# A gated encoder block on one core: root formula, order of the first tiles' products and sharing of the first weights' casts changed

## The chip, the cores and the metric

The kernel runs on one core of a Trainium2 chip. Its engines are named as the profile names them: PE (matrix products, with PEld loading their stationary operand), DVE (vector), ACT (scalar and activations), POOL (GpSimd) and SP (which only issues transfers). The metric is the device time of one execution in microseconds (us). Before the change three runs took 900.99, 902.10 and 902.17 us; their median is 902.1 us.

## The reference

One layer with 1024 tokens and 1024 features: a norm, one wide projection, a window attention branch, a spatial gating branch, two gates, an output projection and a last norm.

```python
def rmsnorm(x, g):
    y = xf * lax.rsqrt(jnp.mean(xf * xf, axis=-1, keepdims=True) + EPS)
    return (y * g.astype(jnp.float32)).astype(x.dtype)

h = rmsnorm(x, norm_g[l])
proj = h @ w_in[l]
q, k, v, za, u, vs, zs, gm = jnp.split(proj, IN_SPLITS, axis=-1)
...
a = (a * jax.nn.silu(za)) @ w_att_out[l]
sgo = chunked_spatial_gating(gelu(u), gelu(vs), sg_w[l], sg_b[l], sg_ln_g[l], sg_ln_b[l])
sgo = (sgo * jax.nn.silu(zs)) @ w_sg_out[l]
ga, gs = jnp.split(jax.nn.sigmoid(gm + b_merge[l]), N_BRANCHES, axis=-1)
x = x + (ga * a + gs * sgo) @ w_o[l]
...
return rmsnorm(x, final_g)
```

## The kernel before

**Products.** Every fp32 factor is split in two parts: a high part (an fp32r copy, made by a cast) and a low part (the source minus the high part, made by a subtraction). A product is then three PE products: high by high, high by low and low by high. On top of that, matrices are cut in 2x2 blocks and multiplied with seven block products in place of eight. That needs sums of weight blocks (`s1` to `s4`) and sums of token blocks (`b11`, `b21`, `t1` and so on).

**The head.** The first stage computes the block `vs` of the projection, with tokens on the partitions. There are eight tiles of 128 tokens. Tiles 0 to 3 go through `first_tile`, tiles 4 to 7 through `second_tile`. For each tile:

- `load_x` brings the tile by a transfer on SP's queue. Tiles 0, 1, 2, 5, 6 and 7 share three buffers `wr`, tiles 3 and 4 lie in `T_t1l`; a later tile's load waits until an earlier tile has left its buffer.
- `scale_of` sums the squares on ACT and calls `rstd_of`, which makes the reciprocal root: a scaled mean on DVE, a root on ACT, a reciprocal and then one step of refinement on DVE.
- `turned_half` scales one half of the tile on DVE (`scalings`) and turns it with four PE transposes into a bank `ps_sc`.
- `form_of` casts the bank into the high part on ACT (`casts`) and subtracts the low part on DVE (`lows`).
- `first_product` issues 24 products of 128x512: twelve of `b11` with the weight block `a11` (bank `ps_mm` or `ps_tp`) and twelve of `b21` with `a12` (bank `ps_o`). Then ACT copies the second bank.

**The first weights.** `a11` and `a12` come in two chunks each (c = 0 to 3), each of two halves of 512 columns. `split_vs` makes their high and low parts. Before the change ACT casts both halves of chunk 0 and all of chunk 3, and POOL casts chunks 1 and 2; DVE subtracts, but for one half of chunk 0, which POOL subtracts.

**The sums of weights.** The blocks `s1`, `s2` and `s4` are made by transfers that add to their destination (`add_on`), issued by POOL: first on `T_t4h`, which becomes `s1`, in two chunks, then on `T_t3h` (`s2`) and `T_t3l` (`s4`), each from the one before. `split_behind` casts and subtracts `s1` into `T_t2h` and `T_t2l`, one cast for each chunk of 1024 columns.

**Order.** A scheduler puts the instructions of each engine into one sequence, which the engine then follows strictly. `after(second, first)` adds an edge that the scheduler must keep; it makes no wait of its own when both stand on one engine. `behind` and `paced` make a real wait. `keep_busy(n)` issues n products on constant data ahead of the first transposes.

**The end.** The last stage multiplies by `w_o`, adds the residual and applies the last norm with `rstd_of`. Its last root uses the option `times_minus_2`, which leaves out one step and takes a gain that was scaled by -0.5 (`g_last`).

Of the kernel before, what the change touches and what calls it, by code (L numbers as in the profile page):

```python
# [24 lines left out]
F32 = mybir.dt.float32  # L25
# [27 lines left out]
def hybrid_tile(  # L53
# [51 lines left out]
    eps_sb = const.tile([P, 1], F32, name="eps_sb")  # L105
    nc.gpsimd.memset(eps_sb[:], EPS)
    zeros = [nc.gpsimd.memset(g_both[:, at : at + 2, :].bitcast(F32), 0.0) for at in (0, 2)]
# [25 lines left out]

    def rstd_of(ss, scale, base=EPS, n=1, times_minus_2=False):

        ve = mtile([P, n], F32, f"st{n}", 16 if n == 1 else 5)
        of_mean.append(nc.vector.tensor_scalar(ve[:], ss, scale, base, op0=ALU.mult, op1=ALU.add))
        rt = mtile([P, n], F32, f"st{n}", 16 if n == 1 else 5)
        of_root.append(nc.scalar.activation(rt[:], ss, AF.Sqrt, bias=eps_sb[:] if base is EPS else base, scale=scale))
        r0 = mtile([P, n], F32, f"st{n}", 16 if n == 1 else 5)  # L140
        nc.vector.reciprocal(r0[:], rt[:])
        e = mtile([P, n], F32, f"st{n}", 16 if n == 1 else 5)
        if n == 1:
            nc.vector.scalar_tensor_tensor(e[:], ve[:], r0[:], r0[:], op0=ALU.mult, op1=ALU.mult)
            if times_minus_2:
                nc.vector.scalar_tensor_tensor(e[:], e[:], 3.0, r0[:], op0=ALU.subtract, op1=ALU.mult)
                return e
        else:
            nc.vector.tensor_mul(e[:], ve[:], r0[:])
            nc.vector.tensor_mul(e[:], e[:], r0[:])  # L150
        nc.vector.tensor_scalar(e[:], e[:], -0.5, 1.5, op0=ALU.mult, op1=ALU.add)
        nc.vector.tensor_mul(e[:], e[:], r0[:])
        return e
# [418 lines left out]
    for n in range(2):  # L572
        for half in range(2):
            spread(n, half)
    keep_busy(9)

# [57 lines left out]
    def form_of(name, t, src, minus=False):  # L634
# [6 lines left out]
        else:  # L641
            casts.append(nc.scalar.copy(hi, src))
            lows.append(nc.vector.tensor_sub(lo, src, hi.bitcast(F32)))

    def split_behind(hi, lo, src):
        after(nc.scalar.copy(hi, src), casts[-1])
        after(nc.vector.tensor_sub(lo, src, hi.bitcast(F32)), lows[-1])

# [67 lines left out]
    def split_vs(c):  # L716
        name = "a11" if c < 2 else "a12"
        raw = two_k(raws[name], c % 2)
        if c < 3:
            hi, lo = pair_of_w()  # L720
        else:
            hi, lo = (mtile([P, D], F32R, "s", 2) for _ in range(2))
        if c in (1, 2):

            for k in range(2):
                nc.gpsimd.tensor_copy(hi[:, half_of(k)], raw[:, k, :])
            first_lows.append(nc.vector.tensor_sub(lo[:], flat(raw), hi[:].bitcast(F32)))  # L727
        elif c:
            first_lows.append(split(hi[:], lo[:], flat(raw)))
        else:  # L730

            for k in range(2):
                ks = half_of(k)
                after(nc.scalar.copy(hi[:, ks], raw[:, k, :]), of_root[0])
                first_lows.append(
                    (nc.gpsimd if k else nc.vector).tensor_tensor(
                        lo[:, ks], raw[:, k, :], hi[:, ks].bitcast(F32), op=ALU.subtract
                    )
                )
        keep_w(name, c % 2, hi, lo)  # L740

    def vs_product(acc, name, t, weight, fresh, last=True, cs=(0, 1), terms=(0, 1, 2)):
        bh, bl = hb[name]
        for c in cs:
            for n in terms:
                for k in (2 * c, 2 * c + 1):
                    wh, wl = vs_w[weight, k]
                    lt = (bh, bh, bl)[n][:, k, tokens(t)]
                    rt = (wh, wl, wh)[n]
                    mm = nc.tensor.matmul(  # L750
                        acc[:],
                        lt,
                        rt,
                        start=fresh and k == 0 and n == 0,
                        stop=k == 3 and n == terms[-1],
                        skip_group_check=True,
                    )
        return mm

    accs = {}  # L760
    t5s = {}

    def first_product(t):
        accs[t] = bank("mm" if t < 2 else "tp")
        m2 = bank("o")
        if t:
            vs_product(accs[t], "b11", t, "a11", True)
            vs_product(m2, "b21", t, "a12", True)
        else:
            vs_product(accs[t], "b11", t, "a11", True, cs=(0,))  # L770
            vs_product(accs[t], "b11", t, "a11", False, cs=(1,), terms=(0, 2, 1))
            vs_product(m2, "b21", t, "a12", True, terms=(0, 2, 1))
        nc.scalar.copy(x_place(0, 0, t), m2[:])

# [3 lines left out]
    def by_s1(t):  # L778
        t5s[t] = bank("o" if t < 2 else "sc")
        mm = vs_product(t5s[t], "t1", t, "s1", True)  # L780
        nc.scalar.mul(x_place(1, 1, t), t5s[t][:], -1.0)
        return mm
# [4 lines left out]
    def keep_t5(t):  # L787
        nc.scalar.copy(x_place(0, 1, t), t5s[t][:])

# [5 lines left out]
    x_in[1] = load_x(1)  # L795
    first_lows = []
# [23 lines left out]
    for c in (2, 3):  # L820
        split_vs(c)
        after(first_lows[c + 1], lows[1])
    after(hi_of[0], casts[1])
    for move in unsplit:
        after(move(), hi_of[0])
    for c in range(2):
# [25 lines left out]
    mm = by_s1(0)  # L852
    load_part("s3", "t4h", 1, 0, mm)
    a22 = [raw_tile(), mtile([P, D], F32, "s", 2)]
# [19 lines left out]
    after(second_tile(6), move)  # L874
    mm = by_s1(1)
    after(second_tile(7), move)
# [19 lines left out]
    split_w("s2", 1)  # L896
    for t in range(4):
        keep_t5(t)

# [981 lines left out]
    g_both = bq()  # L1881
    g_out, g_last = g_both[:, 0:2, :], g_both[:, 2:4, :]
    nc.sync.dma_start(g_out.rearrange("p h n -> p (h n)"), final_g.partition_broadcast(P))
# [7 lines left out]
    for p in range(4):  # L1891
# [10 lines left out]
        def add_and_square(i, half, src, sign):  # L1902
            z = xr[:, 2 * i + half, :]
            pace[0] = (nc.vector.tensor_sub if sign < 0 else nc.vector.tensor_add)(z, z, src)
            ss = mtile([P, 1], F32, "st1", 16)
            nc.scalar.activation(bank("tp")[:], z, AF.Square, accum_out=ss[:])
            if p == 3 and i == half:
                scaled[i, half] = mtile([P, HALF], F32, gtag(), 1, pool)
                gain = (g_last if i else g_out)[:, half, :]
                nc.gpsimd.tensor_tensor(scaled[i, half][:], z, gain, op=ALU.mult)  # L1910
            if i in sq:
                sq[i] = rstd_of(ss[:], 1.0 / D, sq[i][:])
            else:
                nc.vector.tensor_scalar(ss[:], ss[:], 1.0 / D, EPS, op0=ALU.mult, op1=ALU.add)
                sq[i] = ss

        def scale_and_store(i, p=p, t=t, xr=xr, sq=sq, scaled=scaled):
            r = sq[i]
            row = slice((t + i) * P, (t + i + 1) * P)
            for e in range(2):  # L1920
                z = xr[:, 2 * i + e, :]
                if (i, e) in scaled:
# [5 lines left out]
                    continue  # L1928
                gain = (g_last if p == 3 and i else g_out)[:, e, :]
                by_gain = nc.vector.scalar_tensor_tensor(z, z, r[:], gain, op0=ALU.mult, op1=ALU.mult)  # L1930
# [8 lines left out]
        product(acc, ready[n, 3], ob["t2"], False)  # L1939
        copied = nc.scalar.copy(x12[:], acc)  # L1940
        if p == 2:
            after(nc.scalar.mul(g_last, g_out, -0.5), copied)
        if p:
# [44 lines left out]
        for e in range(2):  # L1988
# [7 lines left out]
            if e == 0:  # L1996
                base = mtile([P, 1], F32, "st1", 16)
                nc.vector.scalar_tensor_tensor(base[:], ss[:], 1.0 / D, sq[1][:], op0=ALU.mult, op1=ALU.add)
            else:
                sq[1] = rstd_of(ss[:], 1.0 / D, base[:], times_minus_2=True)  # L2000
        scale_and_store(0)
# [84 lines left out]
```

## Time and profile before

| what | value |
|---|---|
| median of three runs | 902.1 us (900.99 to 902.17) |
| the profiled execution: its time, its span | 900.83 us, 899.0 us |
| around the span (the difference) | 1.8 us |
| busy: PE, PEld, DVE, ACT, POOL | 890.0, 745.2, 683.5, 529.5, 153.6 us |
| granted PE clock, mean | 0.998 |
| from the start to the first transpose's load | 8.13 us |
| first product of tile 0, first product of tile 1 | 9.63 us, 17.26 us |
| last product's end to the end of the span | 892.48 to 899.0 us |

How to read it: the page gives for each engine the time in which it was busy. The timeline gives start, length, engine, line, operation and shape of each group of instructions, and in square brackets how long the engine had been idle and what released it. The chain of waits is followed back from the last instruction. Products on PE overlap, so that one lasts longer (some 0.39 us) than the distance between two of them.

### The profile page before, as it was taken

The page shows a single profiled execution, that of the slowest core. Times are in us where ns is not written, and L with a number is a line of the kernel's source. Part 1 is how long each engine was busy: PE and PEld are TensorE (multiplying, and loading weights), DVE is VectorE, ACT ScalarE, POOL GpSimd, SP SyncE. Part 2 cuts the span into 40 slices and gives each one's busy share as a digit, 9 for nine tenths or more (in the row PEclk, how much of TensorE's full clock was granted, in tenths as well). Part 3 has the DMA queues.
Part 4 walks back from the last instruction along what each step waited for, and adds up shares of the span by engine and source line. Part 5 has one row for each costly group of instructions (what it writes and reads, how often), then busy time and mean ns, then how long its engine had stood idle before and what let it go on. Part 6 is the DMA issues. An engine that isn't in the chain of part 4 may idle for free.

```text
span 899.0 us, 13239 instructions
## 1 busy us (share of the span) xinstructions
PE 890.0 (99%) x4306; PEld 745.2 (83%) x4306; DVE 683.5 (76%) x1248; ACT 529.5 (59%) x1062; POOL 153.6 (17%) x218
## 2 busy tenths in 40 slices
PE   9999999999999999999999999999999999999997
PEld 6888888888888888888888888888888888888885
DVE  7859966666687788888878888647797488479986
ACT  7866533334445567677777776755585376467453
POOL 4322222203030001111210111101121121110012
PEclk9999999999999999999999999999999999999999
DMA  9997888858778767878786789899899789998533
GB/s 331 216 270 205 267 204 174 167 156 263 254 252 281 216 191 213 217 149 209 186 219 227 250 240 202 221 333 361 297 293 370 288 227 258 305 294 287 185 116 119
DMA packets 132750, 213.77 MB, mean 238 GB/s; under 512 B 12777, under 2 KB 61161, under 8 KB 132682
## 3 DMA queue, kind: packets, MB, share of 16 engines
q1 hardware_dynamic: 110072, 149.74, 50.0%
q0 software_dynamic: 22464, 62.93, 31.4%
q8 instruction: 34, 0.56, 0.2%
q14 instruction: 34, 0.28, 0.1%
q10 hardware_dynamic: 146, 0.27, 0.1%
HBM read 147.74 MB, written 86.11 MB: 260 GB/s over the span
## 4 chain that ended last, share of the span: by engine, by line
PE 98%; DVE 1%; ACT 0%; issue 0%; DVEq 0%
PE ps_mm L355 42%; PE ps_o L355 27%; PE ps_tp L355 7%; PE ps_sc L1344 3%; PE ps_sc L355 3%; PE ps_tp L750 2%; PE ps_o L1431 2%; PE ps_o L750 2%; PE ps_tp L1390 2%; PE ps_mm L750 2%; PE ps_tp L1015 2%; PE ps_sc L750 1%; PE ps_sc L629 1%; PE ps_sc L554 1%; DVE wl L727 0%
## 5 line engine op out<-in xcount | busy, mean ns | idle before, releaser
L164 ACT CAST wh<-s 128x1024 fp32r<-128x1024 f32 (+1 forms) x79 | 79.3, 1005 | 91.8 <-PE ps_mm L355 42.0
L165 DVE TENSOR_TENSOR wl<-wr,wh 128x512 fp32r<-128x512 f32 (+1 forms) x77 | 72.0, 937 | 54.1 <-ACT wh L164 53.4
L165 DVE TENSOR_TENSOR wl<-s,wh 128x1024 fp32r<-128x1024 f32 (+1 forms) x79 | 92.9, 1176 | 10.5 <-ACT wh L164 10.4
L164 ACT CAST wh<-wr 128x512 fp32r<-128x512 f32 (+1 forms) x77 | 63.0, 820 | 59.1 <-PE ps_mm L355 30.8
L355 PE MATMUL ps_o<-T_t1h,wh 128*128 128x512 f32 x148 | 58.6, 396 | 0.0
L355 PE MATMUL ps_o<-T_t1h,wl 128*128 128x512 f32 x148 | 57.7, 390 | 0.0
L355 PE MATMUL ps_o<-T_t1l,wh 128*128 128x512 f32 x148 | 57.6, 389 | 0.0
L1359 ACT ACTIVATE pr<-ps_sc,sm 128x192 f32<-128x192 f32 (+2 forms) x128 | 50.9, 410 | 8.3 <-DVE sm L1353 7.3
L355 PE MATMUL ps_mm<-T_t3h,wh 128*128 128x512 f32 x140 | 54.9, 392 | 0.0
L355 PE MATMUL ps_mm<-T_b11h,wh 128*128 128x512 f32 x140 | 54.9, 392 | 0.0
L355 PE MATMUL ps_mm<-T_b11l,wh 128*128 128x512 f32 x140 | 54.7, 391 | 0.0
L355 PE MATMUL ps_mm<-T_t3h,wl 128*128 128x512 f32 x140 | 54.6, 390 | 0.0
L355 PE MATMUL ps_mm<-T_b11h,wl 128*128 128x512 f32 x140 | 54.6, 390 | 0.0
L355 PE MATMUL ps_mm<-T_t2h,wl 128*128 128x512 f32 x140 | 54.6, 390 | 0.0
L355 PE MATMUL ps_mm<-T_t2h,wh 128*128 128x512 f32 x140 | 54.6, 390 | 0.0
L355 PE MATMUL ps_mm<-T_t2l,wh 128*128 128x512 f32 x140 | 54.6, 390 | 0.0
L355 PE MATMUL ps_mm<-T_t3l,wh 128*128 128x512 f32 x140 | 54.5, 389 | 0.0
L355 PE MATMUL ps_mm<-T_t4h,wh 128*128 128x512 f32 x136 | 53.5, 393 | 0.0
L355 PE MATMUL ps_mm<-T_t4h,wl 128*128 128x512 f32 x136 | 53.2, 391 | 0.0
L355 PE MATMUL ps_mm<-T_t4l,wh 128*128 128x512 f32 x136 | 53.0, 389 | 0.0
L309 POOL DMA_DIRECT2D sums<-in_w_dram x40 | 29.4, 930 | 91.8 <-ACT x L373 42.7
L355 PE MATMUL ps_o<-T_b22h,wh 128*128 128x512 f32 x108 | 42.7, 395 | 0.0
(420 smaller groups left out, 2452.0 us busy)
## 6 DMA issues: line engine op xcount, KB each, us to landing
wr<-in_w_dram SPq DMA_DIRECT2D x86, 256.0 KB
sums<-in_w_dram POOLq DMA_DIRECT2D x20, 512.0 KB, 6.5
s<-sums SPq DMA_DIRECT2D x20, 512.0 KB
q_hl<-qhl SPq DMA_DIRECT2D x16, 512.0 KB
q<-q_hl SPq DMA_DIRECT2D x64, 128.0 KB
y_dr<-x POOLq DMA_DIRECT2D x28, 256.0 KB, 7.1
g<-in_w_dram POOLq DMA_DIRECT2D x12, 512.0 KB, 6.5
wr<-in_w_dram SPq DMA_DIRECT2D x11, 512.0 KB
```

Source lines behind the costliest of these rows:

```text
L164: hi_of.append(nc.scalar.copy(hi, src))
L165: return nc.vector.tensor_sub(lo, src, hi.bitcast(F32))
L309: return lambda: paced(nc.gpsimd.dma_start(dst, src, accum_op=op))
L355: nc.tensor.matmul(acc, lt, rt, start=fresh and k == 0 and n == 0, stop=k == 3 and n == 2, skip_group_check=True,)
L554: feed(nc.tensor.matmul(idle[:], ones_r[:, 0:P], ones_r, start=True, stop=True))
L629: turns.append(nc.tensor.transpose(pt[:, i * P : (i + 1) * P], xt[:, k * P : (k + 1) * P], ident[:]))
L750: mm = nc.tensor.matmul(acc[:], lt, rt, start=fresh and k == 0 and n == 0, stop=k == 3 and n == terms[-1], skip_group_check=True,)
L1015: nc.tensor.matmul(pm[:, t * P : (t + 1) * P], xh[:, half * 4 + t, g * P : (g + 1) * P], bias[-1][1][:, g % 4, :], start=True, stop=True,)
L1344: nc.tensor.matmul(sc[:, i, k0:], q_of[:, c, i * P : (i + 1) * P], kt[:, f, k0:], start=f == 0, stop=f == 1,)
L1359: nc.scalar.activation(held_in[c, i], sc[:, i, lo:hi], AF.Exp, bias=nmax[:, c, i : i + 1], scale=-1.0, accum_out=sums[:, c, i : i + 1],)
L1390: nc.tensor.transpose(dst, pr[:, i, block * P : block * P + width], ident[:])
L1431: nc.tensor.matmul(po[:, cs], lt, rt, start=n == 0, stop=n == len(terms) - 1)
```

## The change

**The root.** `rstd_of` makes four times the mean, its root and two reciprocals, and forms root by reciprocal of the mean plus reciprocal of the root. The reciprocal of the mean does not wait for ACT. Per call DVE has one small instruction fewer; `times_minus_2` and `g_last` go, with ACT's scaling of the gain.

**The head's order.** `keep_busy(9)` becomes `keep_busy(6)`. Of tile 0's 24 products the terms with the low part of `a12` (`terms=(1,)`) go behind tile 1's first twelve. The mean, the squares and the casts of tiles 1 and 2 and the subtractions of the weights get other edges, and so do the casts of `s1`, `s4` and `s2` (`highs_behind`, `lows_behind`).

**The first weights.** Chunk 0 is cast second half first. In chunks 2 and 3 ACT casts the first half and POOL the second.

```diff
-    keep_busy(9)
+    keep_busy(6)
-    def rstd_of(ss, scale, base=EPS, n=1, times_minus_2=False):
+    def rstd_of(ss, scale, base=4.0 * EPS, n=1):
-        of_mean.append(nc.vector.tensor_scalar(ve[:], ss, scale, base, op0=ALU.mult, op1=ALU.add))
+        of_mean.append(nc.vector.tensor_scalar(ve[:], ss, 4.0 * scale, base, op0=ALU.mult, op1=ALU.add))
...
+        nc.vector.reciprocal(rv[:], ve[:])
...
         nc.vector.reciprocal(r0[:], rt[:])
...
-            nc.vector.scalar_tensor_tensor(e[:], ve[:], r0[:], r0[:], op0=ALU.mult, op1=ALU.mult)
-            if times_minus_2:
-                nc.vector.scalar_tensor_tensor(e[:], e[:], 3.0, r0[:], op0=ALU.subtract, op1=ALU.mult)
-                return e
+            nc.vector.scalar_tensor_tensor(e[:], rt[:], rv[:], r0[:], op0=ALU.mult, op1=ALU.add)
...
-        nc.vector.tensor_scalar(e[:], e[:], -0.5, 1.5, op0=ALU.mult, op1=ALU.add)
-        nc.vector.tensor_mul(e[:], e[:], r0[:])
         return e
...
+    def very_first_product():
+        accs[0] = bank("mm")
+        sums_of_b21[0] = m2 = bank("o")
+        vs_product(accs[0], "b11", 0, "a11", True, cs=(0,))
+        vs_product(accs[0], "b11", 0, "a11", False, cs=(1,), terms=(0, 2, 1))
+        return vs_product(m2, "b21", 0, "a12", True, terms=(0, 2), stops=False)
...
-    after(of_mean[1], lows[0])
-    after(first_lows[0], scalings[1])
-    after(lows[0], first_lows[0])
+    after(first_lows[1], scalings[1])
+    after(lows[0], first_lows[1])
...
-    after(squares[1], casts[0])
-    after(casts[1], of_root[1])
+    after(of_mean[1], lows[1])
+    after(casts[1], casts[0])
+    after(squares[1], casts[1])
...
+    mm = very_first_product()
     first_tile(1, second)
-    after(scalings[2], first_lows[4])
+    after(turns[8], mm)
+    after(first_lows[3], scalings[3])
...
     first_tile(2)
-    first_product(0)
+    after(squares[2], casts[2])
+    mm = first_product(1, m2_too=False)
+    vs_product(sums_of_b21[0], "b21", 0, "a12", False, terms=(1,), behind_mm=mm)
+    keep_m2(0)
+    vs_product(sums_of_b21[1], "b21", 1, "a12", True)
+    keep_m2(1)
     first_tile(3)
-    first_product(1)
...
     second_tile(4)
+    after(highs_behind[0], of_root[4])
+    after(lows_behind[1], scalings[9])
...
-            gain = (g_last if i else g_out)[:, half, :]
+            gain = g_out[:, half, :]
```

What the scheduler makes of it is seen in the sequences of the engines, at three places.

ACT from the root of tile 0 (`st`) on, with the casts of the first weights (`wh`, `s`), of the turned halves of tile 0 (`T_b11h`, `T_b21h`) and the squares of tile 1 (`wT`). Before:

```order
L139 ACTIVATE st_22_162<-st_20_158,eps_sb 128x1
L734 CAST wh_176<-T_t3h_170 128x512 x2
L642 CAST T_b11h_149<-ps_sc_195 128x4x128
L614 ACTIVATE wT_153,st_30_182<-wr_174 128x1024
L139 ACTIVATE st_32_186<-st_30_182,eps_sb 128x1
L642 CAST T_b21h_151<-ps_sc_203 128x4x128
L164 CAST s_237<-T_t3l_171 128x1024
```

With the change, the same place on ACT:

```order
L143 ACTIVATE st_22_159<-st_20_155,eps_sb 128x1
L731 CAST wh_173<-T_t3h_167 128x512 x2
L641 CAST T_b11h_146<-ps_sc_192 128x4x128
L641 CAST T_b21h_148<-ps_sc_200 128x4x128
L613 ACTIVATE wT_150,st_31_179<-wr_171 128x1024
L143 ACTIVATE st_33_183<-st_31_179,eps_sb 128x1
L741 CAST wh_229<-T_t3l_168 128x512
L741 CAST s_234<-T_t3l_168 128x512
```

The squares of tile 1 stand behind both casts of tile 0, and the one cast of 1024 columns has become two of 512 columns, one for each chunk of `a12`.

PE at the end of tile 0's products (`ps_o_298`) and the start of tile 1's (transposes into `ps_sc` from `wr`, then `ps_mm_354`). Before:

```order
L750 MATMUL ps_o_298<-wh_232,T_b21h_151 128x512 x2
L750 MATMUL ps_o_298<-wh_232,T_b21l_152 128x512 x2
L750 MATMUL ps_o_298<-wl_233,T_b21h_151 128x512 x2
L750 MATMUL ps_o_298<-s_237,T_b21h_151 128x512 x2
L750 MATMUL ps_o_298<-s_237,T_b21l_152 128x512 x2
L750 MATMUL ps_o_298<-s_238,T_b21h_151 128x512 x2
L629 MATMUL ps_sc_250<-ident,wr_174 128x128 x4
L629 MATMUL ps_sc_259<-ident,wr_174 128x128 x4
L750 MATMUL ps_mm_354<-wh_176,T_b11h_149 128x512 x2
```

With the change, from the same product on:

```order
L755 MATMUL ps_o_248<-s_234,T_b21l_149 128x512 x2
L628 MATMUL ps_sc_270<-ident,wr_171 128x128 x4
L628 MATMUL ps_sc_279<-ident,wr_171 128x128 x4
L755 MATMUL ps_mm_317<-wh_173,T_b11h_146 128x512 x2
L755 MATMUL ps_mm_317<-wl_174,T_b11h_146 128x512 x2
L755 MATMUL ps_mm_317<-wh_173,T_b11l_147 128x512 x2
L755 MATMUL ps_mm_317<-wh_207,T_b11h_146 128x512 x2
L755 MATMUL ps_mm_317<-wl_208,T_b11h_146 128x512 x2
L755 MATMUL ps_mm_317<-wh_207,T_b11l_147 128x512 x2
L755 MATMUL ps_o_248<-wl_230,T_b21h_148 128x512 x2
L755 MATMUL ps_o_248<-s_235,T_b21h_148 128x512 x2
```

Four products of tile 0, those with the low parts of `a12` (`wl_230`, `s_235`), have moved behind the twelve of tile 1.

ACT around tile 4's root, with what each instruction waits for in brackets (`DMASW0` is the first chunk of the transfer that adds on `s1`, `DMASW1` the second). `T_t2h` is the high part of `s1`, `xh` takes copies of tile 3's transposes. Before:

```order
L642 CAST T_b11h_149<-ps_sc_337 128x4x128 [waits PE_49]
L139 ACTIVATE st_73_391<-st_71_387,eps_sb 128x1 [waits Activation_49]
L642 CAST T_b21h_151<-ps_sc_346 128x4x128 [waits PE_49]
L646 CAST T_t2h_381<-T_t4h_219 128x1024 [waits DMASW0_49]
L658 COPY xh_119<-ps_sc_337 128x512 [waits DVE_49]
L656 ACTIVATE xh_119<-ps_sc_346 128x512 [waits DVE_49]
L646 CAST T_t2h_381<-T_t4h_219 128x1024 [waits DMASW1_49]
```

With the change:

```order
L641 CAST T_b11h_146<-ps_sc_362 128x4x128 [waits PE_49]
L641 CAST T_b21h_148<-ps_sc_371 128x4x128 [waits PE_49]
L647 CAST T_t2h_379<-T_t4h_216 128x1024 [waits DMASW1_49]
L662 COPY xh_119<-ps_sc_362 128x512 [waits DVE_49]
L660 ACTIVATE xh_119<-ps_sc_371 128x512 [waits DVE_49]
L143 ACTIVATE st_77_389<-st_75_385,eps_sb 128x1 [waits Activation_49]
L647 CAST T_t2h_379<-T_t4h_216 128x1024 [waits DMASW0_49]
```

Tile 4's root (`st_73_391`, now `st_77_389`) stood ahead of both casts of `s1`; it now stands behind the cast that waits for the second chunk and behind two copies. The two chunks have changed places.

More of the change, by code (lines that the diff above doesn't have):

```diff
@@ L643, in form_of @@
             lows.append(nc.vector.tensor_sub(lo, src, hi.bitcast(F32)))
+    highs_behind, lows_behind = [], []
     def split_behind(hi, lo, src):
-        after(nc.scalar.copy(hi, src), casts[-1])
-        after(nc.vector.tensor_sub(lo, src, hi.bitcast(F32)), lows[-1])
+        high, low = nc.scalar.copy(hi, src), nc.vector.tensor_sub(lo, src, hi.bitcast(F32))
+        after(high, casts[-1])
+        after(low, lows[-1])
+        highs_behind.append(high)
+        lows_behind.append(low)
     def first_tile(t, scale=None):
@@ L739, in split_vs, with vs_product @@
                 )
+        else:
+            for k in range(2):
+                to = hi[:, half_of(k)]
+                if c > 1 and k == 0:
+                    first_highs.append(nc.scalar.copy(to, raw[:, k, :]))
+                else:
+                    nc.gpsimd.tensor_copy(to, raw[:, k, :])
+            first_lows.append(nc.vector.tensor_sub(lo[:], flat(raw), hi[:].bitcast(F32)))
         keep_w(name, c % 2, hi, lo)
-    def vs_product(acc, name, t, weight, fresh, last=True, cs=(0, 1), terms=(0, 1, 2)):
+    def vs_product(acc, name, t, weight, fresh, cs=(0, 1), terms=(0, 1, 2), stops=True, behind_mm=None):
         bh, bl = hb[name]
@@ L754, in vs_product @@
                         start=fresh and k == 0 and n == 0,
-                        stop=k == 3 and n == terms[-1],
+                        stop=stops and k == 3 and n == terms[-1],
                         skip_group_check=True,
                     )
+                    if behind_mm is not None:
+                        after(mm, behind_mm)
+                        behind_mm = None
         return mm
@@ L874, in hybrid_tile @@
     after(second_tile(6), move)
+    after(highs_behind[2], of_root[6])
+    after(lows_behind[2], scalings[13])
     mm = by_s1(1)
@@ L896, in hybrid_tile @@
     split_w("s2", 1)
-    for t in range(4):
-        keep_t5(t)
+    kept = [keep_t5(t) for t in range(4)]
+    after(kept[2], hi_of[-1])
     def statistics(t, half):
```

68 lines of the change are left out of this document (33 added, 35 removed).

## The prediction

> **What bounds the kernel now.** I read the page first, then the chain of waits, then the timeline of the first 64 us and of the last 15.
>
> ```profile
> span 899.0 us, 13239 instructions
> PE 890.0 (99%) x4306; PEld 745.2 (83%) x4306; DVE 683.5 (76%) x1248; ACT 529.5 (59%) x1062; POOL 153.6 (17%) x218
> PE 98%; DVE 1%; ACT 0%; issue 0%; DVEq 0%
> 51.32 10.88 PE ps_sc L750 x48
> ```
>
> The chain that ended last is PE for 98% of the span. Where PE has no gap, 48 products take 10.88 us, so 0.2267 us each; this is the price of a product below. A change in the head therefore moves the end by as much as it moves PE's place in its own sequence, and otherwise only the tail counts. PE's stops in the head are these (start, length, engine, line, and in brackets the idle time before and its releaser):
>
> ```profile
> 5.04 3.04 PEld L554 LDWEIGHTS ps_sc<-T_b22l 128*128 128x128 f32 x9
> 8.13 1.02 PEld L629 LDWEIGHTS ps_sc<-ident,wr 128*128 128x128 f32 x8
> 9.63 0.30 PEld L750 LDWEIGHTS ps_mm<-wh,T_b11h 128*128 128x128 f32 x2 [0.47 <-ACT T_b11h L642]
> 13.96 0.30 PEld L750 LDWEIGHTS ps_o<-wl,T_b21h 128*128 128x128 f32 x2 [0.81 <-DVE wl L727]
> 15.93 0.97 PEld L629 LDWEIGHTS ps_sc<-ident,wr 128*128 128x128 f32 x8 [0.29 <-issue]
> 17.26 0.30 PEld L750 LDWEIGHTS ps_mm<-wh,T_b11h 128*128 128x128 f32 x2 [0.37 <-ACT T_b11h L642]
> 29.17 0.42 PEld L629 LDWEIGHTS ps_sc<-ident,T_t1l 128*128 128x128 f32 x4 [0.45 <-ACT T_t2h L646]
> 35.79 0.42 PEld L629 LDWEIGHTS ps_sc<-ident,wr 128*128 128x128 f32 x4 [0.23 <-ACT st L139]
> 36.50 0.42 PEld L629 LDWEIGHTS ps_sc<-ident,wr 128*128 128x128 f32 x4 [0.29 <-issue]
> 48.33 0.42 PEld L629 LDWEIGHTS ps_sc<-ident,wr 128*128 128x128 f32 x4 [0.45 <-issue]
> ```
>
> The reader sees tile 0's transposes at 8.13, its first product at 9.63, a stop of 0.81 for the low part of `a12`, tile 1's transposes at 15.93 and tile 1's product at 17.26. After that the stops are small.
>
> **The start, part by part.** First the root of tile 0 on DVE (start, length):
>
> ```profile
> 6.27 0.22 DVE L144 SCALAR_TENSOR_TENSOR st<-st,st 128x1 f32<-128x1 f32 x1
> 6.52 0.15 DVE L151 TENSOR_SCALAR st<-st 128x1 f32<-128x1 f32 x1
> 6.71 0.16 DVE L152 TENSOR_TENSOR st<-st,st 128x1 f32<-128x1 f32 x1
> 6.96 1.41 DVE L624 SCALAR_TENSOR_TENSOR wr<-wr,st,ps_tp 128x512 f32<-128x512 f32 x2
> ```
>
> The two instructions at 6.52 and 6.71 go; the added reciprocal of the mean runs while ACT makes the root. Scaling starts some 0.38 us earlier, near 6.58, and its first half ends near 7.33. The nine constant products hold PE until 8.08; without three of them they end ahead of 7.4. So the transposes start near 7.45 instead of 8.13 and tile 0's first product near 8.95 instead of 9.63: 0.68 us.
>
> The stop of 0.81 goes, because the four products that need that low part are no longer there: 20 products of 0.2267 from 8.95 end at 13.5. Before that they need the high part of `a12`, each half now on its own engine. I find each high and low part ready 0 to 0.2 us ahead of its product, so the margin is thin. Tile 1's eight transposes then cost the 1.33 us between 15.93 and 17.26, less about 0.1 because ACT is free: its product comes near 14.9. That is 2.36 us ahead of 17.26, with four products (0.91) still owed: a lead of about 1.45 us. The four products repay their time in front of tile 2's transposes.
>
> **Where the lead meets a wait.** The third place in the order decides. Tile 4's root now stands on ACT behind the cast of the second chunk of `s1` and two copies. When does that chunk land? Here are POOL's issue of the transfer, the next thing that waits for it, the landing times of the transfers that touch `T_t4h` (the longest is this one), and ACT before:
>
> ```profile
> 15.75 0.88 POOL L601 DMA_DIRECT2D T_t4h<-in_w_dram  x1 [0.23 <-issue]
> 27.96 0.85 POOL L601 DMA_DIRECT2D T_t3h<-T_t4h  x1 [2.89 <-DMA T_t4h<-in_w_dram]
> DMA to landing us min/median/max: 6.3/8.3/11.7
> 25.10 0.30 ACT L139 ACTIVATE st<-st,eps_sb 128x1 f32<-128x1 f32 x1
> 25.77 1.05 ACT L646 CAST T_t2h<-T_t4h 128x1024 fp32r<-128x1024 f32 x1
> 26.72 0.58 ACT L658 COPY xh<-ps_sc 128x512 f32<-128x512 f32 x1
> 27.20 0.61 ACT L656 ACTIVATE xh<-ps_sc 128x512 f32<-128x512 f32 x1
> 27.68 1.06 ACT L646 CAST T_t2h<-T_t4h 128x1024 fp32r<-128x1024 f32 x1
> 28.62 1.07 ACT L614 ACTIVATE wT<-wr 128x1024 f32<-128x1024 f32 x1
> 28.19 0.75 DVE L624 SCALAR_TENSOR_TENSOR T_t1l<-T_t1l,st,xh 128x512 f32<-128x512 f32 x1
> ```
>
> 15.75 plus 11.7 is 27.45: the second chunk lands there. Before, this cost nothing, since the root ran at 25.10, ahead of both casts. Its cover was that order, and the order is gone. The issue at 15.75 hangs on a load that SP issues as before, so the change does not bring it forward. With the change ACT has done tile 3's two casts near 25.1 and then waits. From start to next start the rows give 0.94 for the cast (27.68 to 28.62) and 0.48 for each copy (26.72 to 27.20 to 27.68): the root runs at 27.45 + 0.94 + 0.96 = 29.35 and ends at 29.65. DVE needs a reciprocal (0.16), one instruction of 0.22 and the scaling of 0.75, with small gaps 1.23 together: 30.88. From the scaling's end at 28.94 to PE's 29.17 lie 0.23; so tile 4's transposes begin at about 31.1.
>
> PE gets there much earlier. By the order it has 71 products and the transposes of tiles 0 to 3 ahead of tile 4's, where it had 66 before. Its old sequence would be at this point at 29.17 plus five products (1.13), so at 30.30; with the lead of 1.45 it arrives near 28.85 and stands for some 2.3 us. The lead is paid into this one wait, and PE is 0.8 us later than before. This doesn't depend on how large the lead is, as long as it is above zero.
>
> **Behind it.** Before, PE lost about 0.3 at 35.79 and 36.50 and 0.15 at 48.33. With the change I follow ACT and DVE on from 31.1 with the rows' durations and find two scalings that end within 0.2 us of PE's need (tiles 5 and 6). I take 0.25 lost, bounded by nothing and by 1.2 (four groups of 0.3). So 0.2 less than before.
>
> **The tail.** The last root and its scaling:
>
> ```profile
> 892.93 0.52 ACT ps_tp L1995 x2
> 893.47 0.30 ACT st L139
> 893.80 0.17 DVE st L141
> 894.00 0.23 DVE st L144
> 894.25 0.17 DVE st L146
> 894.45 0.75 DVE bq L1930
> ```
>
> The step at 894.25 goes; the new reciprocal fits ahead of 893.80. That is 0.19 us off the end. The eight-wide root of the middle stage and ACT's scaling of the gain run under PE's products, and cost or bring nothing; uncovered they would be one or two steps of 0.17 and one of about 1.05 us.
>
> **Sum.** +0.8 (tile 4) - 0.2 (later stops) - 0.2 (tail) = +0.4 us, on a span of 899.0 and a profiled time of 900.83. The median of the runs is 902.1; so 902.5 us.
>
> **Rivals.** 1: the wait does not bite, because the chunk lands before ACT gets there, by 25.1. Then the lead stays: 1.45 + 0.2 + 0.2 = 1.9 us faster, 900.2. For it: PE and ACT would gain all that the start gives. Against it: the landing was at 27.45, and the loads beside it are the same bytes. Each us by which it lands earlier gives back one.
>
> 2: slower. Tile 6's load waits for tile 1's buffer, which PE's transposes free some 2.3 us earlier; if its 512 KB get in front of the add, the chunk lands later, and every us goes to the end, since PE is already waiting. The price comes from how fast transfers moved while the adds were under way (window, length, busy time of PE, PEld, DVE, ACT, POOL, clock, share, GB/s), the range from adds with few loads beside them (tile `T_t3l`):
>
> ```profile
> 16.00:20.00 4.00, 3.87 (x21) 2.94 (x20) 3.08 (x10) 3.70 (x8) 0.63 (x1) 1.00 1.06 356
> DMA to landing us min/median/max: 4.5/4.7/4.9
> ```
>
> At 356 GB/s 512 KB take 1.5 us: 904.0. For it: an add takes 11.7 us among SP's loads and 4.7 without, so loads do hold it up. Against it: tile 5's load was already queued on SP, so the order among SP's loads is the same. [...]
>
> 3: ACT and DVE, pushed together behind the wait, become the bound until tile 7: the 1.2 us of the bound above, 903.5; this stays within what cannot be told.
>
> That the order named in the change is not built as named is no rival: the sequence shows four products moved, not eight, and the sum counts four.
>
> **How the numbers follow.** Forecast with rival 3: 0.55. Rival 1: 0.20. Rival 2: 0.25. The likeliest one's own range is 901.6 to 903.6 (landing 0.6 us either way, later stops 0 to 1.2). Rival 1's time and rival 2's, 900.2 to 904.2, hold eight in ten. A measurement of this kernel tells about 0.2% (1.8 us) from no change: faster than 900.3 is rival 1 (0.20); slower than 903.9 is rival 2 and the forecast's upper edge (0.30); the rest is 0.50.
>
> **What would show it.** Right: first transposes near 7.45; tile 0's product near 8.95 with no stop for `wl` behind it; tile 1's near 14.9; ACT idle near 25 to 27.4, released by the transfer onto `T_t4h`; PEld idle about 2 us ahead of the transposes from `T_t1l` at 31; one step fewer at the end. Wrong: the cast of `T_t2h` starting without a wait near 25 (rival 1), or only at 29 (rival 2); a second stop of over 0.5 us on PE between 31 and 62; tile 1's product later than 16.5, so that the sharing with POOL costs more than it gives.

## The result and the profile after

| | before | changed |
|---|---|---|
| median of 12 runs each | 901.18 us (900.25 to 902.17) | 902.94 us (901.33 to 904.07) |
| ratio, 95% interval | | 1.0019, 1.0010 to 1.0028 |
| profiled execution: time, span | 900.83, 899.0 us | 904.07, 902.3 us |

The changed kernel is 0.19% slower, 1.8 us. Its profiled execution is the slowest of its twelve, 1.1 us above their median; the rows below show why. The page of the changed kernel, and the head of its chain of waits:

```profile
span 902.3 us, 13217 instructions
PE 890.8 (99%) x4303; PEld 746.1 (83%) x4303; DVE 682.3 (76%) x1232; ACT 528.4 (59%) x1062; POOL 153.5 (17%) x218
PE 92%; DMA 4%; DVE 2%; SPq 1%; ACT 0%; issue 0%; POOL 0%; DVEq 0%; ACTq 0%
```

Before, the chain was PE for 98% of the span. Now 4% of it is a transfer, so there is a place where PE does wait. The timeline of PE's weight loads shows the faster start and that place:

```profile
7.58 1.03 PEld L628 LDWEIGHTS ps_sc<-ident,wr 128*128 128x128 f32 x8
9.09 0.30 PEld L755 LDWEIGHTS ps_mm<-wh,T_b11h 128*128 128x128 f32 x2 [0.47 <-ACT T_b11h L641]
13.53 1.03 PEld L628 LDWEIGHTS ps_sc<-ident,wr 128*128 128x128 f32 x8
15.04 0.30 PEld L755 LDWEIGHTS ps_mm<-wh,T_b11h 128*128 128x128 f32 x2 [0.47 <-ACT T_b11h L641]
...
28.38 0.19 PEld L755 LDWEIGHTS ps_o<-s,T_b21l 128*128 128x128 f32 x1
31.06 0.71 PEld L628 LDWEIGHTS ps_sc<-ident,T_t1l 128*128 128x128 f32 x4 [2.50 <-ACT T_t2h L647]
...
31.97 0.76 PEld L755 LDWEIGHTS ps_tp<-wh,T_b11h 128*128 128x128 f32 x2
32.83 0.76 PEld L755 LDWEIGHTS ps_tp<-wl,T_b11h 128*128 128x128 f32 x2
33.68 0.76 PEld L755 LDWEIGHTS ps_tp<-wh,T_b11l 128*128 128x128 f32 x2
34.48 0.42 PEld L755 LDWEIGHTS ps_tp<-wh,T_b11h 128*128 128x128 f32 x2
```

Tile 1's first product stands at 15.04 where it stood at 17.26, with no stop for `wl` before it. Then PE waits 2.50 us ahead of tile 4's transposes. The row names a cast of `T_t2h` as releaser, but what these transposes read is `T_t1l`, which DVE scales with tile 4's root. PE goes on 0.23 us after the end of that scaling, as before the change (28.94 to 29.17 before, 30.83 to 31.06 now). ACT and DVE in the same stretch show the whole row of waits:

```profile
24.91 0.59 ACT L641 CAST T_b21h<-ps_sc 128x512 fp32r<-128x512 f32 x1
27.38 1.05 ACT L647 CAST T_t2h<-T_t4h 128x1024 fp32r<-128x1024 f32 x1 [1.89 <-DMA T_t4h<-in_w_dram]
...
29.30 0.29 ACT L143 ACTIVATE st<-st,eps_sb 128x1 f32<-128x1 f32 x1
```

```profile
29.63 0.16 DVE L145 RECIPROCAL st<-st 128x1 f32<-128x1 f32 x1 [3.41 <-ACT st L143]
...
30.08 0.75 DVE L623 SCALAR_TENSOR_TENSOR T_t1l<-T_t1l,st,xh 128x512 f32<-128x512 f32 x1
```

ACT stands until the second chunk of `s1` lands at 27.38, the root follows at 29.30 behind two copies, the scaling ends at 30.83 and PE goes on at 31.06.

Two more things cost time. The first is seen in the loads above: from 31.97 on six products take 2.51 us, 0.42 each and not 0.2267. The windows (length, busy time of PE, PEld, DVE, ACT, POOL, granted clock, transfer share, GB/s) say why:

```profile
24.00:28.00 4.00, 4.00 (x22) 3.37 (x21) 1.54 (x4) 2.04 (x4) 0.94 (x2) 1.00 1.04 293
28.00:31.00 3.00, 0.99 (x5) 0.49 (x3) 1.30 (x4) 3.00 (x6) 0.77 (x1) 1.00 1.09 218
31.00:34.00 3.00, 2.91 (x9) 2.55 (x10) 2.76 (x4) 1.94 (x5) 0.85 (x1) 0.50 0.82 161
34.00:36.00 2.00, 2.00 (x11) 1.64 (x11) 0.84 (x2) 0.43 (x2) 0.85 (x1) 0.90 1.02 190
```

Behind the stop the granted clock, the share of its full speed at which PE was allowed to run, was 0.50. Over the six products this is 2.51 - 6 x 0.2267 = 1.15 us. The second is a stop after tile 7's transposes, near 54:

```profile
52.22 0.42 PEld L628 LDWEIGHTS ps_sc<-ident,wr 128*128 128x128 f32 x4 [0.17 <-issue]
52.61 0.30 PEld L755 LDWEIGHTS ps_o<-wh,T_b22l 128*128 128x128 f32 x2
52.91 0.58 ACT L641 CAST T_b22h<-ps_sc 128x512 fp32r<-128x512 f32 x1 [3.12 <-PE ps_sc L628]
53.40 0.60 ACT L674 ACTIVATE x<-ps_sc 128x512 f32<-128x512 f32 x1
...
54.05 0.30 PEld L755 LDWEIGHTS ps_sc<-T_t2h,T_t1h 128*128 128x128 f32 x2 [1.14 <-ACT x L674]
```

The product at 54.05 needs a bank `ps_sc` that tile 7's transposes have just filled. ACT must first copy it out, and only two products stand in between. Before, the same product came without a wait; eight products stood between the first half of tile 7's transposes and this product, where now there are two:

```profile
50.93 0.42 PEld L750 LDWEIGHTS ps_sc<-T_t2h,T_t1h 128*128 128x128 f32 x2
```

At this product PE is 54.05 - 50.93 = 3.1 us late, and at the end the span is 3.3 us longer. Up to there both kernels have run the same number of products. So nearly all that this execution lost, it had lost by 54 us.

### The profile page after: what moved, and what is told of

It is laid out like the page before. It is cut to its first block, busy times and chain, and to the rows that moved or that the text cites. A ratio compares the mean times of both kernels' runs of the same rounds, so it can differ in the third digit from the quotient of the medians.

```text
span 902.3 us, 13217 instructions
## 1 busy us (share of the span) xinstructions
PE 890.8 (99%) x4303; PEld 746.1 (83%) x4303; DVE 682.3 (76%) x1232; ACT 528.4 (59%) x1062; POOL 153.5 (17%) x218
## 4 chain that ended last, share of the span: by engine, by line
PE 92%; DMA 4%; DVE 2%; SPq 1%; ACT 0%; issue 0%; POOL 0%; DVEq 0%; ACTq 0%
PE ps_mm L354 40%; PE ps_o L354 25%; PE ps_tp L354 7%; PE ps_sc L1375 3%; PE ps_sc L354 3%; PE ps_o L1462 2%; DMA T_t4h<-in_w_dram 2%; PE ps_tp L755 2%; PE ps_tp L1421 2%; PE ps_mm L755 2%; PE ps_tp L1046 2%; PE ps_o L755 2%; PE ps_sc L755 1%; DMA wr<-in_w_dram 1%; DMA q<-q_hl 1%; DMA q_hl<-qhl 1%
```

## The experiments

Ratios are to the kernel before, measured beside each. The experiments ran in three groups on three chips (the first four; then the products in the wait, the formula alone, the first run with the later loads and the kernel before with them; then the rest), so between groups the ratios say more than the times. No run takes the new sharing of the casts by itself.

**Tile 4's root first.** The cast that waits for the second chunk is put behind the root.

```diff
     after(highs_behind[0], of_root[4])
+    after(highs_behind[1], of_root[4])
```

> The changed kernel with one edge more: the cast of the second chunk of s1 stands behind tile 4's root on ACT. Theory (the long stop of 2.46 us on PE ahead of tile 4's transposes, and the slower products right behind it, come from this cast's wait for its transfer): the root runs near 25.5, the stop falls below 0.5 us, no products at half the granted clock between 31 and 35, and the time falls by 2.0 to 3.5 us against the changed kernel, to 899.5 to 901. Rival (the lead is lost at the next wait anyway): the stop of 1.1 us near 52.7 grows or a new one comes before 62, and the time stays within 0.8 us of 902.9.

The median is 899.77 us, against 901.06 for the kernel before beside it, but the ratio is 1.0004 (0.9982 to 1.0026): seven runs lay at 898.42 to 899.89, below every run of the kernel before beside them (899.97 the lowest), and five at 902.53 to 907.63. The profiled execution, one of the five (902.53), in PE's and ACT's rows:

```profile
28.36 0.42 PEld L628 LDWEIGHTS ps_sc<-ident,T_t1l 128*128 128x128 f32 x4 [0.41 <-ACT T_t2h L647]
67.57 0.59 ACT L806 COPY xh<-ps_sc 128x512 f32<-128x512 f32 x1 [3.45 <-DMA xh<-xh]
72.04 1.03 ACT L163 CAST wh<-T_t4h 128x1024 fp32r<-128x1024 f32 x1
73.48 0.30 PEld L755 LDWEIGHTS ps_mm<-wh,T_t3h 128*128 128x128 f32 x2 [2.53 <-ACT wh L163]
```

The stop for tile 4 is 0.41 and the half clock is gone: the cause of the wait is shown. The stop near 54 is gone too; between 29 and 73 us no stop is longer than 0.62. But PE, now early, meets the next late transfer. ACT waits for an add on `xh` until 67.57, its cast comes at 72.04, and PE stands 2.53 us at 73.48. The theory holds for the wait; the rival holds for part of the runs, at a place past the 62 us that I had named. What the four runs from 904.01 to 907.63 met, at mean clocks of 0.994 to 0.997, no profile shows.

**Tile 7's squares first.** An edge that should bring tile 7's scaling and transposes forward.

```diff
     after(second_tile(7), move)
+    after(highs_behind[2], squares[7])
```

> The changed kernel with one edge more: one cast of s4 stands behind tile 7's squares on ACT, so that tile 7's scaling and transposes come earlier. Theory (the stop of 1.1 us near 52.7 comes from tile 7's transposes standing only two products ahead of the product that waits for their bank): that stop falls below 0.4 us, the long stop near 28.4 stays at about 2.5, and the time falls by 0.7 to 1.1 us, to about 902. Rival (PE only waits elsewhere): another stop of over 0.7 us up to 62 takes its place, time unchanged at 902.9.

902.49 us, ratio 1.0012 (1.0001 to 1.0024). The stop stayed:

```profile
30.41 0.42 PEld L628 LDWEIGHTS ps_sc<-ident,T_t1l 128*128 128x128 f32 x4 [2.11 <-ACT T_t2h L647]
...
50.38 1.05 ACT L647 CAST wh<-T_t3h 128x1024 fp32r<-128x1024 f32 x1
51.33 0.60 ACT L674 ACTIVATE x<-ps_sc 128x512 f32<-128x512 f32 x1
51.98 0.30 PEld L755 LDWEIGHTS ps_sc<-T_t2h,T_t1h 128*128 128x128 f32 x2 [1.39 <-ACT x L674]
```

Six products now stand behind the first half of tile 7's transposes, but the scheduler has put a cast of `s2` (1.05) ahead of the copy that frees the bank. One edge moved the stop's cause, not the stop. The stop for tile 4 (2.11) is there as before; the clock behind it stayed at 1.00 (this row is a window, in the columns given above):

```profile
31.00:34.00 3.00, 3.00 (x17) 2.48 (x16) 3.00 (x5) 2.08 (x4) 0.85 (x1) 1.00 0.51 100
```

Two profiles name the bank's copy as what PE waits for; the expected gain of 0.7 to 1.1 us did not come.

**Both edges.**

> The changed kernel with both edges. Theory (two separate stops add up): 3 to 4.5 us less than the changed kernel, 898.5 to 900, so faster than the kernel before by 1 to 2.5 us. Rival (one takes the other's place): no better than the better of the two alone.

900.61 us, ratio 1.0001 (0.9980 to 1.0021), no better than the first alone. In its profiled execution the second chunk landed later, and a new stop came ahead of tile 5:

```profile
29.31 1.05 ACT L647 CAST T_t2h<-T_t4h 128x1024 fp32r<-128x1024 f32 x1 [1.68 <-DMA T_t4h<-in_w_dram]
35.98 0.42 PEld L628 LDWEIGHTS ps_sc<-ident,wr 128*128 128x128 f32 x4 [1.46 <-ACT st L143]
```

Tile 5's root also stands behind that cast and what follows it. The gains didn't add up: the rival. Why the chunk landed that late, the runs don't show.

**Nine constant products in place of six.** Nothing else moves.

```diff
-    keep_busy(6)
+    keep_busy(9)
```

> The changed kernel with nine constant products at the start in place of six; the order of all else is the same. Theory (the lead of the head is paid into the wait for tile 4, so its size doesn't matter): first transposes 0.6 us later near 8.15, tile 1's product near 15.6, the stop ahead of tile 4's transposes shorter by 0.6 (about 1.8 in place of 2.46), tile 4's transposes at 31.1 as before, time within 0.4 us of the changed kernel's 902.9 or less, if the shorter stop spares the half clock. Rival (the start counts): 0.6 us slower than the changed kernel.

902.44 us, ratio 1.0018 (1.0007 to 1.0029), the changed kernel's own. The start moved less than expected: the first transposes came at 7.78 and tile 1's product at 15.26. In the profiled execution tile 4's transposes came at 30.44, not at 31.1:

```profile
26.76 1.05 ACT L647 CAST T_t2h<-T_t4h 128x1024 fp32r<-128x1024 f32 x1 [1.05 <-DMA T_t4h<-in_w_dram]
30.44 0.42 PEld L628 LDWEIGHTS ps_sc<-ident,T_t1l 128*128 128x128 f32 x4 [1.66 <-ACT T_t2h L647]
```

The stop is 1.66 in place of 2.50, and ends 3.68 us after the cast's start, as in the changed kernel (31.06 - 27.38 = 3.68); only the chunk landed 0.6 earlier in this execution. The second experiment's profile makes the cleaner pair, since its cast started at 26.73, almost as here, behind six constant products. There tile 1's product came 0.48 us earlier (14.78), the stop was 0.45 longer (2.11), and the transposes stood at the same place (30.41, again 3.68 behind the cast's start). So the wait ends when the chunk says, and the start's lead goes into it: shown.

**Products in the wait.** Eight products on old data go into the bank that tile 4's transposes overwrite.

```diff
         pt = bank("sc")
+        if len(turns) == 32:
+            bh = hb_first["b11"][0]
+            for i in range(8):
+                mm = nc.tensor.matmul(
+                    pt[:], bh[:, i % 4, tokens(2)], vs_w["a11", 0][0], start=True, stop=True, skip_group_check=True
+                )
+                before_turns.append(mm)
...
     first_product(2)
+    after(before_turns[0], last_m2[-1])
```

> The changed kernel with eight products on old data (into the bank that tile 4's transposes then overwrite) in front of tile 4's transposes, so that PE works through most of the wait. Later stages keep their work; the order of tiles 5 to 7 shifts a little. Theory (the products after the wait run at half the granted clock because PE stood idle before them): clock 1.00 between 31 and 36, products there 0.23 us apart, no run of the twelve with a mean clock below 0.998, and the time 0.5 to 1.5 us below the changed kernel's 902.9, without its group near 903.8. Rival (the half clock comes by itself at this place): clock 0.50 there again, mean clock 0.996 in about half of the runs, time as the changed kernel or up to 1.8 us more.

903.02 us, ratio 1.0017 (1.0000 to 1.0034). The windows and the next stop:

```profile
28.00:31.00 3.00, 3.00 (x15) 2.49 (x14) 1.96 (x4) 3.00 (x7) 0.11 (x1) 1.00 1.04 206
31.00:34.00 3.00, 2.60 (x17) 2.04 (x16) 2.97 (x7) 1.24 (x3) 0.85 (x1) 1.00 0.60 119
37.45 0.42 PEld L636 LDWEIGHTS ps_sc<-ident,wr 128*128 128x128 f32 x4 [1.02 <-ACT st L143]
```

With PE busy through the wait the clock stayed at 1.00, and ten of eleven runs had a mean clock of 0.998 or more. The time didn't fall, and the profile shows three losses in place of the wait. The eight products held the first half of tile 4's transposes until 30.90, though its scaling had ended at 30.17; the second half, which now follows it directly, waited 0.60; and tile 5's root, with its own wait, gave a stop of 1.02. The theory on the clock agrees, though the profiled executions of the second and fourth experiments kept 1.00 without such products too; its price in us is not shown by this run.

**The formula alone.** The kernel before with the new `rstd_of` and what goes with it.

```diff
-    nc.gpsimd.memset(eps_sb[:], EPS)
+    nc.gpsimd.memset(eps_sb[:], 4.0 * EPS)
...
+        nc.vector.reciprocal(rv[:], ve[:])
...
-            nc.vector.scalar_tensor_tensor(e[:], ve[:], r0[:], r0[:], op0=ALU.mult, op1=ALU.mult)
+            nc.vector.scalar_tensor_tensor(e[:], rt[:], rv[:], r0[:], op0=ALU.mult, op1=ALU.add)
```

> The kernel before with the new root formula alone (with the scaled eps, and without the scaled gain at the end); head, dummies and sharing of casts as before. Theory (the formula is worth its one step in the tail): the last root's step count falls by one, 0.2 us less after the last product, the head's first transposes stay at 8.13 because nine dummies hold PE, time 0.2 to 0.6 us below the kernel before. Rival (the scheduler orders the head otherwise with the new steps and loses by it): stops of over 0.5 us more in the first 62 us, time above the kernel before.

908.78 us, ratio 1.0071 (1.0056 to 1.0087): the rival, and by far more than 0.5. Rows of PE, and a window:

```profile
43.88 0.42 PEld L628 LDWEIGHTS ps_sc<-ident,wr 128*128 128x128 f32 x4 [1.72 <-issue]
72.56 0.30 PEld L749 LDWEIGHTS ps_mm<-wh,T_t2h 128*128 128x128 f32 x2 [2.53 <-ACT wh L163]
73.82 0.50 PEld L749 LDWEIGHTS ps_mm<-wl,T_t2h 128*128 128x128 f32 x2 [0.96 <-DVE wl L164]
72.00:80.00 8.00, 6.93 (x17) 5.13 (x18) 7.25 (x11) 6.49 (x10) 0.69 (x1) 0.57 0.23 69
```

With the shorter root the scheduler put the head together otherwise, with stops at 43.88, 72.56 and 73.82 and a mean clock of 0.57 from 72 to 80. In that window PE was busy for 6.93 us with 17 products, which at 0.2267 each are 3.85, so the clock cost some 3 us. The cast that PE waits for at 72.56 was late because ACT had waited 5.39 us for an add on `xh`, until 68.63 (61.91 before). The first transposes came at 7.57, not at 8.13 as I had expected. The formula's own gain is there: from the first DVE step behind the last product to the end of the last scaling it is 2.57 us, against 2.72 before. No step of the formula is slow: its four DVE rows last 0.14 to 0.22 each.

**The changed head with the old formula.**

```diff
-            nc.vector.scalar_tensor_tensor(e[:], rt[:], rv[:], r0[:], op0=ALU.mult, op1=ALU.add)
+            nc.vector.scalar_tensor_tensor(e[:], ve[:], r0[:], r0[:], op0=ALU.mult, op1=ALU.mult)
+            if times_minus_2:
+                nc.vector.scalar_tensor_tensor(e[:], e[:], 3.0, r0[:], op0=ALU.subtract, op1=ALU.mult)
+                return e
```

> The changed kernel with the old root formula and its scaled gain (head's order, six dummies and sharing of casts as changed). Theory (the change's loss sits in the order on ACT, and the formula brings about 0.2 us in the tail and some 0.2 to 0.4 in the head's wait): the long stop ahead of tile 4's transposes stays, 2 to 3 us, the tail is 0.2 longer, time 903 to 904. Rival (the new formula makes the loss): time back to the kernel before, within 0.5 us, or faster.

903.59 us, ratio 1.0028 (1.0017 to 1.0038). The wait is there and longer:

```profile
27.50 1.05 ACT L648 CAST T_t2h<-T_t4h 128x1024 fp32r<-128x1024 f32 x1 [2.44 <-DMA T_t4h<-in_w_dram]
31.56 0.42 PEld L629 LDWEIGHTS ps_sc<-ident,T_t1l 128*128 128x128 f32 x4 [3.22 <-ACT T_t2h L648]
```

From the cast's start to tile 4's transposes it is now 4.06 us, 0.38 more than with the new formula, and the tail is 2.71 us long, as before. So the loss sits in the head as it was changed and not in the formula. That the formula takes a little off it is seen in these rows of one execution; the ratio doesn't tell it from the changed kernel's 1.0019 (1.0010 to 1.0028).

**Root first, and small loads later.** The first experiment, and the loads of the gating stage's vectors, sinks, weight and bias, which SP issued among the weights, wait for a later product.

```diff
+    after(highs_behind[1], of_root[4])
...
-    behind(nc.sync.dma_start(lg_sb[:], ln_g), mm)
...
     by_s1(2)
-    by_s1(3)
+    mm = by_s1(3)
+    behind(nc.sync.dma_start(lg_sb[:], ln_g), mm)
```

> The kernel with tile 4's root first (the first experiment), and the small loads on SP for the gating stage (its norm vectors, sinks, weight and bias) set behind a later product. Theory (the lead that the first experiment keeps is lost in some runs at the adds on xh, which land late beside those loads): the last add on xh lands before 66 in place of 67.5, ACT's wait of 3.45 us at 67.6 and the PE stop of 2.5 us at 73.5 go, runs above 902 go, median near 899. Rival (the transfers as a whole set that time, or the loads come too late where they are): the spread from 898 to 907 stays, or a stop moves to the next weights, median no better than 899.8.

899.99 us, ratio 0.9983 (0.9975 to 0.9992), with all eleven runs between 899.21 and 901.10. The median of 899 was not reached. Run again, beside the last kernels:

> The kernel with tile 4's root first and the late loads once more, beside the next three on one chip. It should again lie 1 to 2.5 us below the kernel before, with no run over 1.5 us above its median.

899.86 us, ratio 0.9990 (0.9981 to 0.9999), runs from 899.11 to 901.65, the highest 1.8 above the median, where I had allowed 1.5. The waits that the first experiment met, in the first of the two:

```profile
66.37 0.59 ACT L806 COPY xh<-ps_sc 128x512 f32<-128x512 f32 x1 [2.05 <-DMA xh<-xh]
72.28 0.30 PEld L755 LDWEIGHTS ps_mm<-wh,T_t3h 128*128 128x128 f32 x2 [0.59 <-ACT wh L163]
```

The add still comes after 66, so my number was missed, but it is 1.2 earlier, and PE's stop went from 2.53 to 0.59 (0.90 in the second profile). The runs above 902 are gone. By both ratios this kernel is faster than the kernel before, by 0.17% and 0.10%. That the small loads themselves were in the way is not shown: with the edit SP also issues the next four loads of weights (256 KB each) from 42.92 on, where the first experiment's profile has them from 51.78, and no run separates the two.

**The later loads in the kernel before.**

> The kernel before with the same loads set later. Theory (the kernel before is not held by those adds in most runs): time within 0.4 us of the kernel before; only its few runs near 905 may go. Rival (the loads' place alone is worth something or costs): over 0.5 us either way.

902.12 us, ratio 0.9993 (0.9975 to 1.0011): as expected, no gain by itself that these runs could tell from none. In these runs the later loads are worth something only beside tile 4's root first, where PE is early.

**Two variants of that kernel.** Nine constant products, and the edge on tile 7's squares.

> The same kernel as the one run beside it (tile 4's root first, late loads) with nine constant products at the start in place of six; the order of all else is the same. Theory (with the wait for tile 4 gone, the start is passed on to the end): 0.4 to 0.7 us slower than the kernel beside it, where the changed kernel itself lost nothing by the same three products. Rival (another wait takes the lead further on): within 0.2 us of it.

900.63 us, ratio 0.9995 (0.9986 to 1.0004). This is 0.77 above the kernel beside it and a little above what the theory said, but the intervals overlap. The two profiled executions speak for the rival. They differ in the first transposes by 8.07 - 7.88 = 0.19 us, and nothing of this is left at tile 3's transposes (24.01 and 24.02) or at tile 4's (29.25 in both). What separates them comes later: PE's stop for the cast near 73 is 1.75 us here and 0.90 beside it, since the add on `xh` came late again (67.54). The first row is the kernel beside it, the second this one:

```profile
72.59 0.30 PEld L755 LDWEIGHTS ps_mm<-wh,T_t3h 128*128 128x128 f32 x2 [0.90 <-ACT wh L163]
73.45 0.30 PEld L755 LDWEIGHTS ps_mm<-wh,T_t3h 128*128 128x128 f32 x2 [1.75 <-ACT wh L163]
```

So here, too, the start's lead went into a wait, and what the 0.77 comes from stays open.

> The same kernel with the cast of s4 behind tile 7's squares as well. Theory (the stop near 46 to 50 is gone already once the root of tile 4 comes first, so that this edge has nothing to win): within 0.4 us of the kernel beside it. Rival: 0.5 us or more faster by an earlier tile 7.

900.14 us, ratio 0.9982 (0.9966 to 0.9998), 0.3 from the kernel beside it: as expected. Neither profile has a stop above 0.47 us between 46 and 54.

## Why the prediction was right, and where it was off

The time of 902.5 was met within 0.5 us and the sign was as forecast, but the closeness of the time is in part luck. The 0.19% lies just inside the 0.2% that I had set as the bound of no change, though its interval excludes zero. The difference was not met as well: +0.4 forecast, +1.8 measured (0.9 to 2.5 by the interval). The median of three runs that I started from was 0.9 above the median of twelve, and this covered most of the 1.4 that the sum lacked. By steps:

- **The start** held. First transposes 7.58 (forecast 7.45), tile 0's product 9.09 (8.95), no stop for `wl`, tile 1's product 15.04 (14.9). My own terms for the last one give 13.5 + 1.33 - 0.1 = 14.7, not 14.9; the eight transposes cost 1.51 (13.53 to 15.04), so two slips cancelled.
- **The wait** held in every link: landing 27.38 (27.45), root 29.30 (29.35), scaling's end 30.83 (30.88), transposes 31.06 (31.1), stop 2.50 (2.3). The run with tile 4's root first shows that the order makes it, the one with nine constant products that the lead's size goes into it, the one with the old formula that it isn't the formula's. PE was 31.06 - 30.30 = 0.76 late there, against 0.8. That the landing came within 0.1 us was partly luck: I had given it 0.6 either way, and this cast started between 26.72 and 29.31 in the profiles where it waited for the chunk.
- **What follows a stop** was missing from the sum. I priced the stop by its length and let PE go on at 0.2267 a product. The granted clock fell to 0.50 and added 1.15 us. It doesn't fall each time: the profiled executions of the second and fourth experiments had stops of 2.1 and 1.7 and a clock of 1.00, and the first experiment's had one of 2.53 at 73.48 with a clock of 1.00 over 60 to 80. So the length of the stop alone doesn't decide it. Of the changed kernel's twelve runs six had a mean clock of 0.996 or 0.997 and took 903.32 to 904.07, the six at 0.998 or 0.999 took 901.33 to 902.56. That grouping is a hint only, since runs of the kernel before reach 0.997 too; the window above is what shows the half clock. Even the six at the higher clock have a median of 902.4, 1.3 above the kernel before, so the half clock is not all that the sum lacked. In the profile of the changed kernel the clock was 0.50 over 31.0 to 34.0, 0.60 over 34.0 to 34.5 and 1.00 over 34.5 to 35.0; what makes it fall and what brings it back, the runs do not show.
- **The later stops** were mis-sized. I took 0.25 from a bound of 0 to 1.2, by following ACT and DVE on with their rows. The stop of 1.14 at 54 alone was near the upper end. It is the size of rival 3, and a second stop of over 0.5 between 31 and 62, which I had listed as a sign of being wrong. The mechanism is not rival 3's: the product waits for a bank that ACT has not yet copied out. I had followed when tiles 5 and 6 come, and not how many products stand behind tile 7's transposes: two, where eight stood before.
- **The tail** held. From the first DVE step behind PE's last product to the end of the last scaling it was 894.45 + 0.75 - 892.48 = 2.72 and is now 897.71 + 0.75 - 895.88 = 2.58. That is 0.14 less against a forecast of 0.19, with one step fewer:

```profile
895.88 0.42 DVE bq L2022
...
897.45 0.23 DVE st L148
...
897.71 0.75 DVE bq L1961
```

- **Rival 1** (no wait) did not come in any profiled execution of the changed order. **Rival 2** (tile 6's load pushes the chunk back) did not come either: SP issued the loads of tiles 6 and 7 from 14.87 on, not 17.20, and the chunk landed at 27.38.

```profile
14.87 6.58 SPq L539 DMA_DIRECT2D wr<-in_x_dram  x2
```

Why the earlier loads left it where it was, no run shows. The chunk doesn't always land then: in the third experiment its cast started at 29.31, which was my sign for rival 2, and what delayed it there is open. The 4.7 us that I set against 11.7 came from adds whose source is the tile `T_t3h` and not DRAM, so they don't show by themselves what the loads cost.

- **The range** was added up wrongly: 902.5 + 0.6 + (1.2 - 0.25) is 904.05 and not 903.6, and rival 2's time was 904.0 and not 904.2. The measured median lies inside either way.

The added sum for the profiled execution is thus 0.76 + 1.15 + 1.14 = 3.05, with smaller stops, gains and the tail making up the rest to 3.3. The 1.8 between the medians can't be divided up in this way from one profile.

## What to carry to other kernels

Where a program is built by a scheduler, price a change by the sequence that comes out: here the formula cost 6 us where the scheduler made another order of it and in the changed head shortened a wait by 0.38 us and the tail by 0.14 (one profile each), and one edge on the engine that waits for a transfer took a stop from 2.50 us to 0.41. A lead on the bounding engine is only worth what the next late transfer leaves of it (a lead of 0.48 us became 0.45 more of a stop here), so follow the transfers on to the place where the next one is late, and try whether what can come later is in its way. And price a stop on PE with what its clock may do behind it, not by its length alone: here 1.15 us came on top of 2.50, and in other profiles nothing.

## What was not expected

Behind a stop of 2.50 us the granted clock was 0.50 over 3.0 us and 0.60 over the next 0.5, and behind stops of 1.66, 2.11 and even 2.53 it was 1.00. In the run of the formula alone the mean clock was 0.57 over the 8 us around two stops of 2.53 and 0.96. With the old formula in the changed head, behind a stop of 3.22 that ended at 31.56, two products still took 0.47 us (their loads, from 32.28 on) and the next two 0.77; the clock was 0.80 over 31 to 34 and 0.50 over 34 to 36. The scatter differed as well: the first experiment ran from 898.42 to 907.63, and with the small loads moved (on another chip) from 899.21 to 901.10. That this comes from PE's slack to the transfer is a guess.
